# Seven block products for sixteen contraction tiles instead of eight in the second and third pair of output tiles of a down projection

## The chip, the cores and the metric

The kernel runs on one core of one Trainium2 chip. The metric is the device time of one execution in microseconds (us). Three runs of the kernel before took 891.26, 890.07 and 891.31 us, median 891.26.

## The reference

The reference is one layer of a hybrid encoder block over 512 positions of width 1024: two recurrent branches (RWKV-7 and Gated DeltaNet) on one input projection, a gated merge, an output projection with residual, then a gated feed-forward part and a final norm. The change touches only the last product of the feed-forward part:

```python
h = rms_norm(x, norm2_g[l]) @ ffn_up[l]              # 512 x 1024 @ 1024 x 5632
h = causal_depthwise_conv(h, ffn_conv_w[l])
h_gate, h_up = _split(h, (FFN_HIDDEN, FFN_HIDDEN))   # 2816 each
x = x + (jax.nn.silu(h_gate) * h_up) @ ffn_down[l]   # 2816 x 1024
return rms_norm(x, final_g)
```

Everything is float32.

## The kernel before

Activations lie transposed: channels on the 128 partitions, the 512 positions along the free axis. The hidden width 2816 is 22 contraction tiles, the output width 1024 is 8 output tiles, taken in four pairs (`down_pair`, i = 0 to 3).

Each float32 operand is split in two: hi, a rounded copy that ScalarE (ACT) writes, and lo, the rest, subtracted by VectorE (DVE) or GpSimd (POOL). A product is three matmuls: lo weights by hi data, hi by hi, hi by lo. All three add up in PSUM.

The contraction tiles 0 to 7 (four pairs, `NPAIR`) are multiplied by a scheme of Strassen's kind (`seven`): a pair of output tiles, a pair of contraction tiles and the two halves of the positions (a and b, 256 each) make a 2 x 2 by 2 x 2 block product, done with seven block products instead of eight. The weight side needs the blocks A11, A12, A22 and four sums S1 to S4, the data side the blocks B11, B21, B22 and four sums T1 to T4. `pair_operands` builds the data side while the up projection runs (eight tiles, in `uh` and `ul`, `eh`, `el` and the lora buffers). `pair_weights` builds the weight side, for two contraction pairs at a time: one raw buffer of 128 x 1024, filled by two transfers of 256 KB, four sums of 256 columns, four splits. The split weights go into `u2h` and `u2l`, the inputs of the up projection, which are free by then; they hold two such sets.

The contraction tiles 8 to 21 are multiplied plainly (`plain`), with matmuls of 512 columns; their weights come by `unit` and `halves_of`, in parts of 512 columns, through two raw buffers and a ring of four hi and four lo tiles (`HB`).

The order of the work is drawn up ahead of the run by the framework: each instruction goes to its engine's queue by its priority and by when a planner takes its inputs and buffers to be ready; on the chip each engine then runs its queue in that order, with semaphores. Weight loading and splitting is traced at high priority. In the first and third output pair the plain tiles come first and the seven products behind them; in the second and fourth it is the other way round, so that the seven products of two neighbours stand back to back. After the products the blocks are added up out of PSUM (`V`, `W`) into `x1`, and `total` adds the accumulated rows. The last output tile is done in two halves, each with its normalisation and its part of the output transfer.

The lines that the steps touch: `halves_of` (158 hi, 160 lo), `split` (203, 204), `pair_operands` (1018), `pair_weights` (1044 transfers, 1048 sums, 1057 hi, 1058 lo), `mm` (1089), the block sums (1108, 1109), `total` (1135, 1138), the last tile's norm (1163 to 1172).

Of the kernel before, what the change touches and what calls it, by code (L numbers as in the profile page):

```python
# [9 lines left out]
F32 = mybir.dt.float32  # L10
F32R = mybir.dt.float32r
BF16 = mybir.dt.bfloat16
AF = mybir.ActivationFunctionType
ALU = mybir.AluOpType
PSUM = bass.MemoryType.PSUM

T = 512
D = 1024
KD = D // 128
# [3 lines left out]
HB = 4  # L23
TAGS = {"T": 4, "P": 3, "T2": 2}
# [8 lines left out]
NJ = HID // 128  # L33
NPAIR = 4
# [62 lines left out]
class Body:  # L97
# [938 lines left out]
        self.pairs[i] = B  # L1036


    def pair_weights(self, m, s):
        nc = self.nc  # L1040
        with self.tc.high_priority():
            raw = self.stream.tile([128, 1024], F32, tag="raw", name=self.nm("raw"), bufs=2)
            for i in range(2):
                nc.sync.dma_start(out=raw[:, i * 512:i * 512 + 512], in_=self.a["ffn_down"][m + i][:, s * 512:s * 512 + 512])
            A = raw.rearrange("p (m c i t) -> p m i c t", m=2, c=2, i=2)
            s12, s34 = [self.t("P") for _ in range(2)]
            v = lambda t: t.rearrange("p (s c t) -> p s c t", s=2, c=2)
            tt = lambda out, x, y, op: nc.vector.tensor_tensor(out=out, in0=x, in1=y, op=op)
            p = 4 * (self.sets % 2)
            self.sets += 1  # L1050
            h, l = [[t[:, p + q, :] for q in range(4)] for t in (self.u2h, self.u2l)]

            def parts(q, src, w, eng):
                hq, lq = h[q][:, 0:w], l[q][:, 0:w]
                if len(src.shape) == 3:
                    hq, lq = [x.rearrange("p (c t) -> p c t", c=2) for x in (hq, lq)]
                nc.scalar.activation(hq, src, AF.Copy)
                eng.tensor_tensor(out=lq, in0=src, in1=hq.bitcast(F32), op=ALU.subtract)

            parts(0, raw[:, 0:512], 512, nc.gpsimd)  # L1060
            tt(v(s12)[:, 0], A[:, 1, 0], A[:, 1, 1], ALU.add)
            tt(v(s12)[:, 1], v(s12)[:, 0], A[:, 0, 0], ALU.subtract)
            parts(3, A[:, 1, 1], 256, nc.vector)
            tt(v(s34)[:, 1], A[:, 0, 1], v(s12)[:, 1], ALU.subtract)
            tt(v(s34)[:, 0], A[:, 0, 0], A[:, 1, 0], ALU.subtract)
            parts(1, s12, 512, nc.vector)
            parts(2, s34, 512, nc.gpsimd)
        w = {}
        for n, q, f in (("A11", 0, lambda c: 2 * c), ("A12", 0, lambda c: 2 * c + 1), ("A22", 3, lambda c: c),
                        ("S1", 1, lambda c: c), ("S2", 1, lambda c: 2 + c), ("S3", 2, lambda c: c), ("S4", 2, lambda c: 2 + c)):  # L1070
            w[n] = [tuple(t[q][:, f(c) * 128:f(c) * 128 + 128] for t in (h, l)) for c in range(2)]
        return w


    def down_pair(self, i, act, acc):
        nc, tc = self.nc, self.tc
        x1 = self.x1
        H = T // 2
        a, b = slice(0, H), slice(H, T)
        m1 = 2 * i  # L1080
        end = i == KD // 2 - 1
        tags = "DDAA" if i % 2 == 0 else "ABBB"
        rows = [self.bank_of(t) for t in tags[0:2]]
        pc, pd = [self.bank_of(t) for t in tags[2:4]]
        started = set()


        def mm(bank, out, w, x, stop=False):
            nc.tensor.matmul(out, w, x, start=bank not in started, stop=stop)  # L1089
            started.add(bank)  # L1090

        def seven():
            X = {"X1": ("c", pc, a), "X6": ("c", pc, b), "X5": ("d", pd, a), "X7": ("d", pd, b),
                 "X2": ((0, False), rows[0], a), "X3": ((0, False), rows[0], b), "X4": ((1, False), rows[1], a)}
            for s in range(NPAIR // 2):
                w = self.pair_weights(m1, s)
                for A, B, x in (("A11", "B11", "X1"), ("A12", "B21", "X2"), ("A22", "T4", "X4"), ("S1", "T1", "X5"),
                                ("S2", "T2", "X6"), ("S4", "B22", "X3"), ("S3", "T3", "X7")):
                    for c in range(2):
                        (wh, wl), (xh, xl) = w[A][c], self.pairs[2 * s + c][B]  # L1100
                        fin = s == NPAIR // 2 - 1 and c == 1
                        bank, ps, cols = X[x]
                        mm(bank, ps[:, cols], wl, xh)
                        mm(bank, ps[:, cols], wh, xh)
                        mm(bank, ps[:, cols], wh, xl, stop=fin and (x in ("X6", "X7") or i % 2 == 0 and x in ("X3", "X4")))
            V, W = self.t(), self.t()
            with tc.high_priority():
                tt = lambda out, x, y: nc.vector.tensor_tensor(out=out, in0=x, in1=y, op=ALU.add)
                nc.scalar.activation(V[:, a], pc[:, a], AF.Copy)
                tt(V[:, b], pc[:, b], V[:, a])  # L1110
                tt(W[:, a], pd[:, b], V[:, b])
                tt(V[:, b], pd[:, a], V[:, b])
                tt(W[:, b], pd[:, a], W[:, a])
                for j, t in ((0, V), (1, W)):
                    tt(x1[:, m1 + j, :], t, x1[:, m1 + j, :])

        def plain(j, cols=None):
            ps = rows[j]
            for k0, w in ((8, 8), (16, 6)):
                parts = self.unit(self.a["ffn_down"][m1 + j][:, k0 * 128:(k0 + w) * 128], w * 128)  # L1120
                for q, (wh, wl, n) in enumerate(parts):
                    for part, y in ((wl, 0), (wh, 0), (wh, 1)):
                        for k in range(n):
                            kk = k0 + 4 * q + k
                            wk, x = part[:, k * 128:k * 128 + 128], act(kk)[y]
                            fin = kk == NJ - 1 and y == 1 and i % 2 == 1

                            fresh = j == 1 and i % 2 == 1 and q + k + y == 0 and k0 == 8 and part is wl
                            for s in [cols] if cols else [a, b] if fresh else [slice(0, T)]:
                                mm((j, cols == b), ps[:, s], wk, x[:, s], stop=fin)  # L1130

        def total(m, ps, cols=slice(0, T)):
            x = x1[:, m, cols]
            with tc.high_priority():
                nc.vector.tensor_tensor(out=x, in0=ps[:, cols], in1=x, op=ALU.add)
            if m < KD - 1:
                self.sumsq(acc, x, m == 0)
                nc.scalar.activation(x, x, AF.Copy, scale=self.vec("final", m))

        if i % 2 == 0:  # L1140
            plain(0)
            plain(1)
            seven()
            for j in range(2):
                total(m1 + j, rows[j])
            return
        seven()
        plain(0)
        total(m1, rows[0])
        if not end:  # L1150
            plain(1)
            total(m1 + 1, rows[1])
            return

        for cols in (a, b):
            if cols == b:
                rows[1] = self.bank_of("D")
            plain(1, cols)
            m = KD - 1
            total(m, rows[1], cols)  # L1160
            x = x1[:, m, cols]
            sq, r, pn = self.t(), self.t(), self.bank_of("A" if cols == a else "D")
            nc.scalar.activation(sq[:, 0:H], x, AF.Square)
            nc.tensor.matmul(pn[:, 0:H], self.con("ones"), acc[:, cols], start=True, stop=False)
            nc.tensor.matmul(pn[:, 0:H], self.con("ones"), sq[:, 0:H], start=False, stop=True)
            nc.scalar.activation(x, x, AF.Copy, scale=self.vec("final", m))
            nc.scalar.activation(r[:, 0:H], pn[:, 0:H], AF.Sqrt, bias=self.eps("norm"), scale=1.0 / D)
            nc.vector.reciprocal(r[:, 0:H], r[:, 0:H])
            for k0, k1 in OUTG:
                xo = x1[:, k0:k1, cols]  # L1170
                nc.vector.tensor_tensor(out=xo, in0=xo, in1=r[:, 0:H].unsqueeze(1).broadcast_to([128, k1 - k0, H]), op=ALU.mult)
                nc.sync.dma_start(out=self.o["outT"][k0:k1].rearrange("k p t -> p k t")[:, :, cols], in_=xo)

    def mlp(self):
        nc = self.nc
# [3 lines left out]
        H = T // 2  # L1179
# [3 lines left out]
        lo = [el[:, x, :] for x in range(4)]  # L1183
# [1 line left out]
            lo += [t[:, x * H:x * H + H] for x in range(n)]  # L1185
        self.ext = [([eh[:, i, x, :] for x in range(3)], lo[3 * i:3 * i + 3]) for i in range(NPAIR)]
        self.pairs = {}
        self.sets = 0
        acc = self.g2
        act = lambda j: (self.uh[:, j, :], self.ul[:, j, :]) if j < 8 else (ah[:, j - 8, :], al[:, j - 8, :])  # L1190
        held = None
# [67 lines left out]
```

## Time and profile before

| | before |
|---|---|
| median of three runs | 891.26 us |
| the profiled execution | 889.34 us |
| its span, first to last instruction | 887.6 us |
| TensorE (PE) matmul busy | 854.3 us, 96% |
| VectorE (DVE) busy | 653.5 us, 74% |
| ScalarE (ACT) busy | 466.0 us, 53% |
| GpSimd (POOL) busy | 210.3 us, 24% |
| down projection, first to last matmul start | 759.3 to 877.3 us |

Times inside the profile are us from the span's start. Matmuls are pipelined: their durations overlap, so a stream of them is priced by the distance from one start to the next. Idle time is put down to whatever released the instruction that ended it ("<-").

### The profile page before, as it was taken

Reading aid. Unit: us, or ns where it says so; the run is one execution under the profiler, and the core shown is the slowest. Engines: PE = TensorE matmul, PEld = TensorE weight load, DVE = VectorE, ACT = ScalarE, POOL = GpSimd, SP = SyncE. Lnnn points to the kernel's source line nnn. Section 1 sums busy time; section 2 is a strip of 40 time slices with the busy share of each in tenths; the row PEclk is TensorE's granted clock in tenths of the full one; section 3 lists DMA queues with packets and bytes.
Section 4 is the critical chain, followed back from the end, with each engine's and each line's share of the span. In section 5 each row is a group of like instructions: output and inputs, shape, how many; then the busy total and the mean of one; then the engine's idle time right before and its main releaser. Section 6 shows DMA issues by size and latency. Waiting matters only on the chain.

```text
span 887.6 us, 13504 instructions
## 1 busy us (share of the span) xinstructions
PE 854.3 (96%) x5046; PEld 679.3 (77%) x5046; DVE 653.5 (74%) x1247; ACT 466.0 (53%) x905; POOL 210.3 (24%) x189
## 2 busy tenths in 40 slices
PE   8989999999999899999999999999999999999996
PEld 4867677766777677668788878888888888898895
DVE  6899897973899978944577448998866666573665
ACT  7745357666543677573544455554444444443333
POOL 2231123111111221111122212223222222342431
PEclk9999999999999999999999999999999999999998
DMA  7321222212112211136153223332323332332333
GB/s 265 115 89 59 73 71 73 69 57 68 48 60 72 71 50 60 60 109 213 49 194 113 95 72 95 96 95 98 116 95 95 95 96 89 111 104 82 104 87 132
DMA packets 29746, 84.25 MB, mean 95 GB/s; under 512 B 3312, under 2 KB 5488, under 8 KB 29680
## 3 DMA queue, kind: packets, MB, share of 16 engines
q1 hardware_dynamic: 29680, 83.39, 29.6%
q8 instruction: 40, 0.66, 0.3%
q14 instruction: 26, 0.21, 0.1%
HBM read 77.61 MB, written 5.77 MB: 94 GB/s over the span
## 4 chain that ended last, share of the span: by engine, by line
PE 68%; DVE 16%; ACT 6%; issue 3%; POOL 0%; DVEq 0%; ACTq 0%; POOLq 0%
PE D L185 43%; PE D L1089 5%; PE A L1089 4%; PE B L1089 3%; PE B L185 2%; DVE invN L565 2%; PE A L185 2%; DVE invY L567 2%; DVE P L771 1%; DVE lo L160 1%; DVE R L531 1%; DVE BK L510 1%; DVE BK L515 1%; ACT hi L158 1%; PE B L663 1%
## 5 line engine op out<-in xcount | busy, mean ns | idle before, releaser
L160 POOL TENSOR_TENSOR lo<-raw,hi 128x512 fp32r<-128x512 f32 x124 | 170.6, 1376 | 578.4 <-ACT hi L158 577.2
L158 ACT ACTIVATE hi<-raw 128x512 fp32r<-128x512 f32 x248 | 152.7, 619 | 181.4 <-PE D L185 87.2
L185 PE MATMUL D<-uh,lo 128*128 128x512 f32 x384 | 160.5, 418 | 2.7 <-DVE R L375 1.4
L185 PE MATMUL D<-uh,hi 128*128 128x512 f32 x384 | 151.4, 395 | 0.0
L185 PE MATMUL D<-u2h,lo 128*128 128x512 f32 x352 | 137.9, 392 | 0.0
L185 PE MATMUL D<-u2h,hi 128*128 128x512 f32 x352 | 137.8, 392 | 0.0
L160 DVE TENSOR_TENSOR lo<-raw,hi 128x512 fp32r<-128x512 f32 x124 | 88.2, 711 | 46.3 <-ACT hi L158 45.7
L185 PE MATMUL D<-ul,hi 128*128 128x512 f32 x384 | 109.1, 406 | 0.0
L185 PE MATMUL D<-u2l,hi 128*128 128x512 f32 x352 | 95.1, 392 | 0.0
L185 PEld LDWEIGHTS D<-uh,lo 128*128 128x128 f32 x384 | 72.2, 188 | 21.3 <-issue 3.1
L1006 DVE SCALAR_TENSOR_TENSOR P<-T,vecs,P 128x511 f32<-128x511 f32 x88 | 81.8, 929 | 6.9 <-ACT P L1004 2.6
L185 PEld LDWEIGHTS D<-uh,hi 128*128 128x128 f32 x384 | 72.3, 188 | 14.6 <-issue 1.0
L185 PEld LDWEIGHTS D<-ul,hi 128*128 128x128 f32 x384 | 69.3, 188 | 16.3 <-issue 1.0
L185 PEld LDWEIGHTS D<-u2h,hi 128*128 128x128 f32 x352 | 66.1, 188 | 14.9 <-issue 0.2
L185 PEld LDWEIGHTS D<-u2h,lo 128*128 128x128 f32 x352 | 66.1, 188 | 14.7 <-issue 0.2
L185 PEld LDWEIGHTS D<-u2l,hi 128*128 128x128 f32 x352 | 66.1, 188 | 14.1
L1003 DVE TENSOR_TENSOR T<-D,acc 128x512 f32<-128x512 f32 x44 | 30.2, 686 | 32.0 <-PE D L185 28.2
L565 DVE TENSOR_TENSOR invN<-invA,invY 128x60 f32<-128x60 f32 (+24 forms) x124 | 39.6, 319 | 3.0
L1004 ACT ACTIVATE P<-T,vecs 128x512 f32<-128x512 f32 x44 | 31.7, 721 | 16.5 <-DVE T L1003 14.5
L567 DVE TENSOR_TENSOR invY<-invY,invN 128x60 f32<-128x60 f32 (+24 forms) x124 | 32.3, 260 | 3.0
L771 DVE SCALAR_TENSOR_TENSOR P<-D,vecs,P 128x511 f32<-128x511 f32 (+2 forms) x36 | 26.7, 742 | 0.8 <-ACT P L769 0.7
L1195 ACT ACTIVATE P<-P 128x512 f32<-128x512 f32 x22 | 13.7, 624 | 21.0 <-DVE P L1006 21.0
(437 smaller groups left out, 1556.5 us busy)
## 6 DMA issues: line engine op xcount, KB each, us to landing
raw<-w_in SPq DMA_DIRECT2D x44, 512.0 KB, 3.6
raw<-ffn_up SPq DMA_DIRECT2D x44, 512.0 KB, 3.5
raw<-ffn_down SPq DMA_DIRECT2D x9, 512.0 KB, 3.5
raw<-w_out SPq DMA_DIRECT2D x8, 512.0 KB, 3.5
raw<-ffn_down SPq DMA_DIRECT2D x16, 256.0 KB, 2.9
spill<-T SPq DMA_DIRECT2D x14, 256.0 KB, 2.0
R<-spill SPq DMA_DIRECT2D x14, 256.0 KB, 3.9
raw<-ffn_down SPq DMA_DIRECT2D x9, 384.0 KB, 3.1
```

The lines of the kernel that those rows point to most:

```text
L158: nc.scalar.activation(hi[:, 0:w], raw[:, o:o + w], AF.Copy)
L160: self.on(str(self.halves % 4)).tensor_tensor(out=lo[:, 0:w], in0=raw[:, o:o + w], in1=hi[:, 0:w].bitcast(F32), op=ALU.subtract)
L185: nc.tensor.matmul(ps, t[:, w[k]], x[k][p], start=(first and i == 0 and q == 0), stop=(last and i == len(parts) - 1 and q == len(seq) - 1))
L510: nc.vector.scalar_tensor_tensor(out=bkh[h][s, :, sb, :], in0=q(K, s, h), scalar=self.hkk[s, hp:hp + 1], in1=q(at, s, h), op0=ALU.mult, op ...
L565: nc.vector.tensor_tensor(out=w, in0=rows[:, t, 0:t].unsqueeze(2).broadcast_to([128, t, n]), in1=Ym[:, t, c:G].unsqueeze(1).broadcast_to([ ...
L567: nc.vector.tensor_tensor(out=Ym[:, 0:t, c:G], in0=Ym[:, 0:t, c:G], in1=w, op=ALU.add)
L771: nc.vector.scalar_tensor_tensor(out=cv[:, sh:], in0=ps[:, 0:T - sh], scalar=w(3 - sh), in1=cv[:, sh:], op0=ALU.mult, op1=ALU.add)
L1003: nc.vector.tensor_tensor(out=h, in0=ps, in1=self.acc2, op=ALU.mult)
L1004: nc.scalar.activation(cv, h, AF.Copy, scale=w(2))
L1006: nc.vector.scalar_tensor_tensor(out=cv[:, sh:], in0=h[:, 0:T - sh], scalar=w(2 - sh), in1=cv[:, sh:], op0=ALU.mult, op1=ALU.add)
L1089: nc.tensor.matmul(out, w, x, start=bank not in started, stop=stop)
L1195: nc.scalar.activation(g, g, AF.Silu)
```

## The change

- `late_operands` is new. For the contraction tiles 8 to 15 (four more pairs) it adds hi and lo back together, forms T1 to T4 with four subtractions of 256 columns and splits them into `u2h` and `u2l`. B11, B21 and B22 are the tiles that are there already. It is traced in the first output pair, between `plain(0)` and `seven()`.
- The second and third output pair take sixteen contraction tiles by seven products (two sets of four pairs) and six plainly; the first and the fourth stay at eight and fourteen.
- `pair_weights` makes sets of four contraction pairs. It loads one row of 512 KB for each of the two output tiles, each into a raw buffer of its own (both are used), forms four sums of 512 columns (S3 in place in the raw buffer), and splits each of the seven products' weights into a hi and a lo tile of the ring of four. DVE makes four of the seven lo tiles, POOL three.
- The seven products come in the order A11, A12, S1, S2, S3, S4, A22, each over four contraction pairs.
- The first output pair runs `plain(0)`, the seven products, `plain(1)`; the other three run the seven products first.

The diff, cut to its core:

```diff
+    def late_operands(self, i, act):
...
+        k = 2 * i
+        tt = lambda out, x, y, op: nc.vector.tensor_tensor(out=out, in0=x, in1=y, op=op)
+        g = []
+        for q in range(2):
+            g.append(self.work.tile([128, T], F32, tag="BK", name=self.nm("gu"), bufs=2))
+            h, l = act(k + q)
+            tt(g[q], h.bitcast(F32), l.bitcast(F32), ALU.add)
+        t = [self.work.tile([128, T], F32, tag="T2", name=self.nm("late"), bufs=TAGS["T2"]) for _ in range(2)]
+        tt(t[0][:, a], g[0][:, b], g[0][:, a], ALU.subtract)
+        tt(t[1][:, a], g[1][:, b], g[0][:, b], ALU.subtract)
+        tt(t[0][:, b], g[1][:, b], t[0][:, a], ALU.subtract)
+        tt(t[1][:, b], g[1][:, a], t[0][:, b], ALU.subtract)
+        p = 2 * i - 2 * NPAIR
+        B = {}
+        for q in range(2):
+            h, l = self.u2h[:, p + q, :], self.u2l[:, p + q, :]
+            self.split(h, l, t[q])
...
     def pair_weights(self, m, s):
...
-            raw = self.stream.tile([128, 1024], F32, tag="raw", name=self.nm("raw"), bufs=2)
             for i in range(2):
-                nc.sync.dma_start(out=raw[:, i * 512:i * 512 + 512], in_=self.a["ffn_down"][m + i][:, s * 512:s * 512 + 512])
+                raw = self.stream.tile([128, 1024], F32, tag="raw", name=self.nm("raw"), bufs=2)
+                nc.sync.dma_start(out=raw, in_=self.a["ffn_down"][m + i][:, s * 1024:s * 1024 + 1024])
...
+            S1, S2, S4 = [four(self.t("P")) for _ in range(3)]
+            S3 = A[1, 0]
...
+            for n, B, src, o in (("A11", "B11", A[0, 0], "X1"), ("A12", "B21", A[0, 1], "X2"), ("S1", "T1", S1, "X5"),
+                                 ("S2", "T2", S2, "X6"), ("S3", "T3", S3, "X7"), ("S4", "B22", S4, "X3"), ("A22", "T4", A[1, 1], "X4")):
+                if n == "S1":
+                    tt(S1, A[1, 0], A[1, 1], ALU.add)
+                    tt(S2, S1, A[0, 0], ALU.subtract)
+                    tt(S3, A[0, 0], A[1, 0], ALU.subtract)
+                    tt(S4, A[0, 1], S2, ALU.subtract)
+                hi = self.stream.tile([128, 512], F32R, tag="hi", name=self.nm("hi"), bufs=HB)
+                lo = self.stream.tile([128, 512], F32R, tag="lo", name=self.nm("lo"), bufs=HB)
+                nc.scalar.activation(four(hi), src, AF.Copy)
+                (nc.gpsimd if n in ("A11", "S3", "A22") else nc.vector).tensor_tensor(
+                    out=four(lo), in0=src, in1=four(hi).bitcast(F32), op=ALU.subtract)
...
     def down_pair(self, i, act, acc):
...
+        sets = range(2) if 0 < i < KD // 2 - 1 else range(1)
+        K0 = 8 * len(sets)
...
-            for k0, w in ((8, 8), (16, 6)):
+            for k0, w in ((8, 8), (16, 6))[len(sets) - 1:]:
...
-        if i % 2 == 0:
+        if i == 0:
             plain(0)
-            plain(1)
-            seven()
-            for j in range(2):
-                total(m1 + j, rows[j])
-            return
+            for p in range(NPAIR, 2 * NPAIR):
+                self.late_operands(p, act)
         seven()
-        plain(0)
+        if i:
+            plain(0)
         total(m1, rows[0])
```

## Rows read from the trace of the kernel before

**Rows 1.** Busy time by stretch; the columns are named in the first row.

```profile
core 0: us, PE busy (x) PEld busy (x) DVE busy (x) ACT busy (x) POOL busy (x), PEclk, DMA share, GB/s
740.00:759.30 19.30, 19.30 (x86) 15.82 (x85) 12.52 (x17) 8.91 (x14) 5.38 (x4) 1.00 0.32 101
...
759.30:788.50 29.20, 29.20 (x170) 25.73 (x169) 17.41 (x30) 12.22 (x22) 12.32 (x9) 1.00 0.33 104
```

**Rows 2.** Chain of waits from 740 us: start, us, what.

```profile
759.48 19.23 PE D L1089 x84
...
866.59 4.96 PE B L1089 x42
...
871.57 0.43 DVE x L1135
```

**Rows 3.** Waits of PE from 759 us on: us in total, times, longest.

```profile
PE D L1165 <- ACT T L1163: 0.7, 1, 0.7
```

**Rows 4.** Timeline of PE, first pair: start, us, engine, line, operation.

```profile
759.32 0.39 PE L1089 MATMUL D<-ah,lo 128*128 128x512 f32 x1
...
778.54 0.28 PE L1089 MATMUL A<-uh,u2l 128*128 128x256 f32 x1
...
788.49 0.28 PE L1089 MATMUL B<-uh,u2l 128*128 128x256 f32 x1
```

**Rows 5.** Timelines of ACT, DVE, POOL and SP: weight splits and transfers.

```profile
762.31 0.63 ACT L158 ACTIVATE hi<-raw 128x512 fp32r<-128x512 f32 x1 [1.34 <-PE D L1089]
765.67 0.69 DVE L160 TENSOR_TENSOR lo<-raw,hi 128x512 fp32r<-128x512 f32 x1 [0.71 <-ACT hi L158]
768.52 1.30 POOL L160 TENSOR_TENSOR lo<-raw,hi 128x512 fp32r<-128x512 f32 x1 [4.10 <-ACT hi L158]
760.12 0.41 DVE L160 TENSOR_TENSOR lo<-raw,hi 128x256 fp32r<-128x256 f32 x1
760.60 0.33 SPq L169 DMA_DIRECT2D raw<-ffn_down  x1
766.43 0.80 SPq L1044 DMA_DIRECT2D raw<-ffn_down  x2
769.03 0.63 ACT L1057 ACTIVATE u2h<-raw 128x512 fp32r<-128x512 f32 x1 [0.59 <-DMA raw<-ffn_down]
783.59 0.33 SPq L169 DMA_DIRECT2D raw<-ffn_down  x1
787.10 0.63 ACT L158 ACTIVATE hi<-raw 128x512 fp32r<-128x512 f32 x1 [2.71 <-DMA raw<-ffn_down]
```

**Rows 6.** Timeline of DVE, data operands of the fourth contraction pair.

```profile
611.27 0.69 DVE L204 TENSOR_TENSOR ul<-gu,uh 128x512 fp32r<-128x512 f32 x1
611.87 0.42 DVE L1018 TENSOR_TENSOR t<-gu,gu 128x256 f32<-128x256 f32 x1
612.20 0.68 DVE L204 TENSOR_TENSOR ul<-gu,uh 128x512 fp32r<-128x512 f32 x1
```

**Rows 7.** Timelines of DVE and POOL where both have work.

```profile
778.37 0.67 DVE L1058 TENSOR_TENSOR u2l<-P,u2h 128x512 fp32r<-128x512 f32 x1
778.85 2.35 POOL L1058 TENSOR_TENSOR u2l<-P,u2h 128x512 fp32r<-128x512 f32 x1 [2.37 <-ACT u2h L1057]
...
779.64 0.41 DVE L1048 TENSOR_TENSOR P<-raw,P 128x256 f32<-128x256 f32 x1
...
837.47 1.34 POOL L1058 TENSOR_TENSOR u2l<-P,u2h 128x512 fp32r<-128x512 f32 x1 [2.03 <-ACT u2h L1057]
837.58 1.51 DVE L1048 TENSOR_TENSOR P<-P,raw 128x256 f32<-128x256 f32 x1
...
849.21 1.47 POOL L1058 TENSOR_TENSOR u2l<-P,u2h 128x512 fp32r<-128x512 f32 x1
849.45 0.41 DVE L1108 TENSOR_TENSOR T<-A,T 128x256 f32<-128x256 f32 x1
```

**Rows 8.** Timeline of DVE, the last hidden tile.

```profile
761.00 1.54 DVE L1006 SCALAR_TENSOR_TENSOR P<-T,vecs,P 128x511 f32<-128x511 f32 x2 [0.46 <-ACT P L1004]
```

More of the change, by code (lines that the diff above doesn't have):

```diff
@@ L1036, in pair_operands @@
         self.pairs[i] = B
+    def late_operands(self, i, act):
+        nc = self.nc
+        H = T // 2
+        a, b = slice(0, H), slice(H, T)
+        k = 2 * i
[15 more added lines that the diff above has]
+            self.split(h, l, t[q])
+            for n, c in zip((("T1", "T2"), ("T3", "T4"))[q], (a, b)):
+                B[n] = (h[:, c], l[:, c])
+        for n, q, c in (("B11", 0, a), ("B21", 1, a), ("B22", 1, b)):
+            B[n] = tuple(x[:, c] for x in act(k + q))
+        self.pairs[i] = B
@@ L1039, in pair_weights @@
     def pair_weights(self, m, s):
         nc = self.nc
+        A = {}
+        w = []
         with self.tc.high_priority():
-            raw = self.stream.tile([128, 1024], F32, tag="raw", name=self.nm("raw"), bufs=2)
             for i in range(2):
-                nc.sync.dma_start(out=raw[:, i * 512:i * 512 + 512], in_=self.a["ffn_down"][m + i][:, s * 512:s * 512 + 512])
-            A = raw.rearrange("p (m c i t) -> p m i c t", m=2, c=2, i=2)
-            s12, s34 = [self.t("P") for _ in range(2)]
@@ L1047, in pair_weights @@
-            v = lambda t: t.rearrange("p (s c t) -> p s c t", s=2, c=2)
-            tt = lambda out, x, y, op: nc.vector.tensor_tensor(out=out, in0=x, in1=y, op=op)
[L1049 to L1071, printed above, removed]
+                raw = self.stream.tile([128, 1024], F32, tag="raw", name=self.nm("raw"), bufs=2)
@@ new lines, in pair_weights @@
+                nc.sync.dma_start(out=raw, in_=self.a["ffn_down"][m + i][:, s * 1024:s * 1024 + 1024])
+                v = raw.rearrange("p (c i t) -> p i c t", c=4, i=2)
+                A[i, 0], A[i, 1] = v[:, 0], v[:, 1]
+            four = lambda t: t.rearrange("p (c t) -> p c t", c=4)
+            S1, S2, S4 = [four(self.t("P")) for _ in range(3)]
+            S3 = A[1, 0]
+            tt = lambda out, x, y, op: nc.vector.tensor_tensor(out=out, in0=x, in1=y, op=op)
+            for n, B, src, o in (("A11", "B11", A[0, 0], "X1"), ("A12", "B21", A[0, 1], "X2"), ("S1", "T1", S1, "X5"),
[10 more added lines that the diff above has]
+                    out=four(lo), in0=src, in1=four(hi).bitcast(F32), op=ALU.subtract)
+                w.append((B, o, hi, lo))
@@ L1094, in seven @@
                  "X2": ((0, False), rows[0], a), "X3": ((0, False), rows[0], b), "X4": ((1, False), rows[1], a)}
[L1095 to L1102, printed above, removed]
+            for s in sets:
+                for B, x, hi, lo in self.pair_weights(m1, s):
+                    bank, ps, cols = X[x]
+                    for c in range(4):
+                        wh, wl = [t[:, c * 128:c * 128 + 128] for t in (hi, lo)]
+                        xh, xl = self.pairs[4 * s + c][B]
+                        fin = s == sets[-1] and c == 3
                         mm(bank, ps[:, cols], wl, xh)
                         mm(bank, ps[:, cols], wh, xh)
-                        mm(bank, ps[:, cols], wh, xl, stop=fin and (x in ("X6", "X7") or i % 2 == 0 and x in ("X3", "X4")))
+                        mm(bank, ps[:, cols], wh, xl, stop=fin and x in (("X6", "X7") if i else ("X6", "X7", "X3")))
             V, W = self.t(), self.t()
@@ L1125, in plain @@
                             wk, x = part[:, k * 128:k * 128 + 128], act(kk)[y]
-                            fin = kk == NJ - 1 and y == 1 and i % 2 == 1
-                            fresh = j == 1 and i % 2 == 1 and q + k + y == 0 and k0 == 8 and part is wl
+                            fin = kk == NJ - 1 and y == 1 and i + j > 0
+                            fresh = j == 1 and q + k + y == 0 and k0 == K0 and part is wl
                             for s in [cols] if cols else [a, b] if fresh else [slice(0, T)]:
@@ L1187, in mlp @@
         self.pairs = {}
-        self.sets = 0
         acc = self.g2
```

## The prediction

> **What bounds the kernel now.** I read the stages first [rows 1]: before and in the down projection TensorE (PE) is busy for the whole of each stretch at a granted clock of 1.00 (2.4 GHz), while VectorE (DVE) and GpSimd (POOL) together are busy for as long as the stretch in the first two output pairs' plain tiles and products. The chain of waits [rows 2] says the same from the end backwards: from 759 us to 871.6 us it is matmuls alone; behind them stands the normalisation of the last output tile, which the change leaves as it is. PE's own list of waits from 759 us on has one entry, 0.7 us, and it lies in that tail [rows 3]. So in this stretch the end moves only by matmul time, and by whatever newly fails to be ready for PE.
>
> The matmuls are priced by start to start, since their durations overlap. 84 matmuls of 512 columns start between 759.32 and 778.54: 228.8 ns each. 84 of 256 columns start between 778.54 and 788.49: 118.5 ns each [rows 4]. Half the columns cost 4.1 ns more than half the time.
>
> **Step 1, matmuls: -2.05 us.** Eight contraction tiles (four pairs) of one pair of output tiles cost 2 x 8 x 3 = 48 matmuls of 512 columns, 10.98 us. As seven products they are 4 x 7 x 3 = 84 of 256 columns, 9.95 us. The saving is 1.03 us, for two pairs of output tiles 2.06; two plain runs now begin with a split first matmul (0.01 us each). No other matmul is added or removed. The Trainium skill ("TensorE: Matmul & The Clock Gate", Back-to-back issue gap) puts warm spacing at columns / 2.4 GHz plus 2.5 ns: estimated 109.2 and 215.8 ns, and a saving of 1.19 us per output pair, 2.4 in all; both rows are slower than it says and the rows decide.
>
> **Step 2, weight sets of four pairs: +0.9 us.** One product of a set is now 12 matmuls, 1.42 us, a set 9.95 us. Its weights pass through the ring of four hi and lo tiles that the plain runs use, where before a whole set stood ready in u2h and u2l. A new hi tile can be written when the product four places earlier is through; an ACT copy starts about 0.25 us after the last such matmul (part over at 762.06, copy at 762.31, 0.63 us), the lo subtraction takes 0.69 us on DVE or 1.30 on POOL [rows 5]. From slot to lo tile that is about 2.2 us where 4.27 (three products) are there: hidden inside a set, and from plain to set.
>
> What is late is the turn from one set to the next. The two raw buffers hold both weight rows of a set. The second row is read until the last product, A22, is split. A22 needs the slot of S1, the third product: free at 3 x 1.42 + 0.25 = 4.5 us after the set's start; copy to 5.15, POOL to 6.5. Then SP issues the next 512 KB at 6.6 (0.07 us after the releasing lo, 760.60 behind 760.53), which is there 3.5 us later (issued 783.59, its reader starts 787.10) [rows 5]: at 10.1. Then DVE forms four sums of 512 columns at 0.60 each, in the order of the code, before S1's lo: 12.5, and with 0.69 and a handover 13.2. PE wants S1 after the next set's A11 and A12, at 9.95 + 2.84 = 12.8. That is 0.45 us late, at the two places where a set follows a set (inside the second and the third output pair): 0.9 us. Bounds: nothing, if the data comes after 2.6 us as the first 256 KB piece did (issued 766.43, reader at 769.03); up to 1.5 us each if POOL's lo of A22 is held by DVE as below. I take the middle value because its row is of the same size of transfer. Turns from a set to plain tiles are covered: the first row's buffer is free early.
>
> **Step 3, late operands: +0.7 us.** Per contraction pair two additions, four half-width subtractions and two splits: DVE starts such 512-wide operations 0.60 us apart and 256-wide ones 0.34 apart [rows 6], so 2 x 0.60 + 4 x 0.34 + 2 x 0.60 = 3.76 us, 15.0 for four; ACT's eight copies (5 us) find room, as ACT is busy 12.2 of 29.2 us there. The question is DVE and POOL. When both read SBUF they exclude each other: a POOL subtraction of 1.3 us lasts 2.35 while DVE runs four such operations from 778.37 to 780.05 behind each other, and a DVE one of 0.41 started behind POOL's at 837.47 lasts 1.51, to just after POOL's end; one that reads PSUM (849.45) still takes 0.41 beside POOL [rows 7]. The two engines' SBUF work must therefore be added up. From 759.3 to the first set of the second output pair's S1 (788.5 + 2.84 = 791.4, 32.1 us) stand in line:
> the last hidden tile 2.8 (1.54 for two operations [rows 8], a product and a split at 0.6 to 0.7); the end of plain(0)'s weights 0.4; the first set, 8 DVE operations x 0.60 + 3 of POOL x 1.30 = 8.7; late operands 15.0 less what runs earlier; plain(1)'s weights 2 x 1.30 + 0.60 + 0.34 = 3.5; two additions into x1 1.2; of the next set A11, A12, four sums and S1's lo 4.9.
> The first late pair (2.56 us until its splits, which must wait for u2h and u2l) and the additions of the second (1.20) need only tiles 8 to 11 and free buffers, so they can lie in DVE's gaps before 759 (DVE 12.5 and POOL 5.4 busy of 19.3 us [rows 1] leave 1.4 free; five such stretches pass after tile 11 is there): 3.8. The sum is 36.5 - 3.8 = 32.7 for 32.1; with 0.1 for handovers I take 0.7. Behind that S1 nothing more is lost: what is left of its set, the next set's A11 and A12 and one addition ask 6.3 of 7.1 us. Bounds: nothing, if handovers overlap a little more; and above, if nothing runs early (+3.8) and PSUM reads (0.69 + 4 x 0.34 + 2 x 0.69 = 3.4 us in this stretch) find no cover, 7.9 us. I take the low side, because the operand code of the earlier pairs did fill DVE's row without a gap when it was ready [rows 6] and because PSUM reads go beside POOL [rows 7].
>
> **Sum.** -2.05 + 0.9 + 0.7 = -0.45 us. The profiled execution took 889.34 us (span 887.6 and 1.7 around it), so 888.9 by its measure; it lies 1.9 below the median of the runs, 891.26, and on that scale the forecast is 890.8.
>
> **Rivals.** *Clean gain.* The turn and the late operands are both hidden: -2.05, 889.2. For it: PE waits nowhere in this stretch today although the sets of the first two output pairs stood back to back with DVE and POOL together busy for 29.7 of 29.2 us (both counts hold waiting) [rows 1]; one POOL subtraction fewer per set of four also relieves both. Against: today's double set in u2h and u2l gives the lead that is now given up.
> *DVE and POOL overrun (slower).* The late operands don't start before 759, or stand in DVE's queue ahead of the lo tiles of the first sets, which wait behind them in order: A12's, S1's, S2's and S4's lo, and POOL's A22 behind DVE's run. Then 36.5 us of work meet 32.1: 4.4 us of PE waiting, at the end of the first set, in plain(1) or at the second output pair's first set. With the turn's 0.9: -2.05 + 0.9 + 4.4 = +3.25, 894.5; with uncovered PSUM reads 897.9. It makes the kernel slower from the point where the work ahead of that S1 exceeds 33.3 us (32.1 + 2.05 - 0.9). Against: gaps before 759. The Trainium skill ("SBUF — State Buffer", SBUF: two separate sides) states that whichever of the two engines starts first keeps the shared ports for its whole instruction and the other blocks fully; the trace agrees (1.51 for 0.41), and in the 2.35 us case POOL was held over several instructions.
> *It does less than it says.* If 256-column matmuls of the late pairs came at more than 130.7 ns (10.98 / 84) the saving would be gone: then +1.6, 892.9. Against: all 84 spacings of rows 4 are even; for it nothing.
>
> **How the numbers follow.** A measurement of this kernel can tell about 0.2%, 1.8 us, from no change. The clean gain just exceeds that: chance 0.2. The forecast, with its own range of 889.6 to 893.0, has 0.47, the failed saving 0.03: both are within 0.2%. The overrun has 0.3; nearly all of it is slower by more than 0.2%. So faster 0.2, same 0.5, slower 0.3. The range that holds the time 8 times in 10 takes in the clean gain and most of the overrun: 889.0 to 895.5.
>
> **What would show it.** Step 1: 168 more matmuls of 256 columns and 96 fewer of 512 (but the split ones), at the spacings above. Step 2: PE idle some 0.4 us before S1's lo of the second set, in the second and third output pairs, released by DVE, and ahead of it DVE's sums released by the raw transfer. Step 3: DVE rows of the additions before 759 us, and little PE idle time between 769 and 800 us. Wrong would be: idle PE of several us in that stretch behind lo tiles (overrun); no idle PE at all (clean gain); a wait at any other turn, from a set to plain tiles or at a PSUM bank, which I have at nothing since the banks of one output pair are read out a whole pair before they return.

## The result and the profile after

The changed kernel takes 896.06 us, the median of four runs (895.68 to 896.72), against 890.66 us for the kernel before (four runs, 889.38 to 891.31). The ratio is 1.0064 with a 95% interval of 1.0047 to 1.0081: 5.4 us slower. The time lies just above the range of 889.0 to 895.5, in the span of the rival that was called overrun (894.5, up to 897.9).

| | before | after |
|---|---|---|
| the profiled execution | 889.34 us | 896.72 us |
| its span | 887.6 us | 894.9 us |
| first matmul of the down projection | 759.3 us | 761.4 us |
| from there to the span's end | 128.3 us | 133.5 us |
| matmul instructions | 5046 | 5120 |

Of the 7.3 us between the two spans, 2.1 are there by 548 us already (the first data operand of L1018 starts at 548.4, before at 546.3), ahead of the change's first instruction at 626 us: they are a difference between two executions (TensorE's granted clock is 0.89 from 60 to 75 us and 0.83 from 225 to 235 us in the profile of after, and 1.00 in both stretches of before's). So only the last stretch is compared: 133.5 against 128.3, +5.2 us, close to the 5.4 of the medians. This length, called the segment below, is the span less the start of the first down-projection matmul in the same profile.

Start with what PE waits for, in the profile after, from 740 us on (columns: us in total, times, longest). [rows 3] had the ACT line alone, and it is still there in the tail; the other five are new.

```profile
PE A L1113 <- POOL lo L1091: 2.2, 1, 2.2
PE A L1113 <- DVE lo L1091: 0.8, 1, 0.8
PE D L1186 <- ACT T L1184: 0.7, 1, 0.7
PE D L1113 <- ACT ah L203: 0.6, 1, 0.6
PE D L1113 <- DVE al L204: 0.5, 1, 0.5
PE B L1113 <- DVE lo L1091: 0.4, 1, 0.4
```

The timeline of PE in the profile after (start, us, engine, line, operation, and in brackets the idle time and its releaser) says where three of them are. It answers to [rows 4].

```profile
769.64 0.39 PE L1113 MATMUL D<-ah,lo 128*128 128x512 f32 x1
770.59 0.50 PE L1113 MATMUL D<-ah,lo 128*128 128x512 f32 x1 [0.56 <-ACT ah L203]
...
772.34 0.50 PE L1113 MATMUL D<-al,hi 128*128 128x512 f32 x1 [0.55 <-DVE al L204]
772.67 0.28 PE L1113 MATMUL A<-uh,lo 128*128 128x256 f32 x1
...
778.17 0.28 PE L1113 MATMUL A<-lora_l,hi 128*128 128x256 f32 x1
780.63 0.39 PE L1113 MATMUL A<-eh,lo 128*128 128x256 f32 x1 [2.18 <-POOL lo L1091]
...
782.01 0.41 PE L1113 MATMUL A<-eh,lo 128*128 128x256 f32 x1
782.23 0.41 PE L1113 MATMUL A<-eh,hi 128*128 128x256 f32 x1
...
785.10 0.28 PE L1113 MATMUL D<-eh,lo 128*128 128x256 f32 x1
```

The pauses are the distances from start to start beyond the usual ones (0.229 and 0.117 us): 0.72 + 0.11 us at 770.59 and 0.71 + 0.10 at 772.34 (the second figure is the slower first matmul behind each pause), and 2.34 + 0.10 at 780.63. From 781.6 us on, 0.9 us behind that pause, the matmuls come 0.213 us apart instead of 0.117, until 784.8. Busy time by stretch in the same profile, answering to [rows 1], with the columns named there:

```profile
740.00:761.40 21.40, 21.40 (x96) 17.54 (x94) 16.45 (x22) 10.93 (x18) 5.54 (x4) 1.00 0.32 93
761.40:780.60 19.20, 15.94 (x91) 13.30 (x89) 19.16 (x35) 9.68 (x17) 7.32 (x3) 1.00 0.19 56
780.60:785.10 4.50, 4.47 (x25) 4.47 (x26) 4.16 (x7) 1.26 (x2) 3.10 (x2) 0.62 0.32 87
785.10:795.00 9.90, 9.90 (x53) 8.42 (x52) 6.03 (x11) 3.56 (x6) 2.58 (x2) 1.00 0.36 106
```

In the second stretch DVE is busy for 19.16 of 19.20 us and PE for only 15.94. In the third, PE has a granted clock of 0.62, which is mostly the 1.2 GHz level, soon after a pause of 2.34 us: 24 distances took 4.47 us instead of 2.81.

The chain of waits of after (start, us, what), which answers to [rows 2], shows the big pause and the first turn from set to set (`P` and `raw` at L1080 are the weight sums).

```profile
775.04 5.55 POOL lo L1091
...
780.63 2.23 PE A L1113 x12
...
801.25 1.31 POOL lo L1091
802.58 3.41 DMA raw<-ffn_down
...
806.09 0.70 DVE P L1080
...
808.71 2.31 DVE lo L1091 x2
...
811.06 3.10 PE B L1113 x24
```

One POOL subtraction of 1.3 us ([rows 5]) takes 5.55. It is the lo tile of S3 in the first set, issued at 775.04, while PE asks for it at 778.3. DVE's timeline in after says what it stood beside, and how late the last hidden tile was (its product at 769.20, its split at 771.60).

```profile
764.42 0.68 DVE L204 TENSOR_TENSOR u2l<-late,u2h 128x512 fp32r<-128x512 f32 x1
...
769.20 0.68 DVE L1217 TENSOR_TENSOR P<-P,P 128x512 f32<-128x512 f32 x1
...
771.60 0.68 DVE L204 TENSOR_TENSOR al<-P,ah 128x512 fp32r<-128x512 f32 x1
...
775.02 0.68 DVE L1044 TENSOR_TENSOR gu<-ah,al 128x512 f32<-128x512 f32 x1
775.62 0.41 DVE L1044 TENSOR_TENSOR late<-gu,late 128x256 f32<-128x256 f32 x1
...
777.76 0.68 DVE L1091 TENSOR_TENSOR lo<-P,hi 128x512 fp32r<-128x512 f32 x1
...
779.04 0.41 DVE L1044 TENSOR_TENSOR late<-gu,late 128x256 f32<-128x256 f32 x1
779.48 1.37 DVE L1044 TENSOR_TENSOR late<-gu,late 128x256 f32<-128x256 f32 x1
```

From 775.02 to 779.04 each DVE instruction starts 0.34 or 0.60 us after the one before it, with no pause, and all read two operands from SBUF. The next one starts 0.44 us later, at 779.48, and takes 1.37 us instead of 0.41; POOL's ends at 780.58. The last hidden tile is split at 771.60, 10.2 us after the down projection's first matmul. In before that was 4.6 (763.96 against 759.32):

```profile
763.96 1.00 DVE L204 TENSOR_TENSOR al<-P,ah 128x512 fp32r<-128x512 f32 x1 [0.70 <-ACT ah L203]
```

There, between that first matmul and this split, DVE's queue held one weight lo of 0.41 us (760.12, [rows 5]) and no weight sum beside the tile's own work. In after it held late operands, three of the four weight sums and a weight lo as well.

All of it together: -2.05 (fewer matmul columns) - 0.75 (504 matmuls of 256 columns, now 117.0 ns apart instead of 118.5) + 1.64 (last hidden tile) + 2.44 + 1.56 (POOL's S3, and the half clock behind it: 4.47 - 2.81 less the 0.10 already counted) + 1.0 and 1.3 (the turns at 809.36 and 838.69) = +5.1, against 5.2 in the segments.

### The profile page after: what moved, and what is told of

Same layout as the page of the kernel before. It is cut to its first block, busy times and chain, and to the rows that moved or that the text cites. A ratio compares the mean times of both kernels' runs of the same rounds, so it can differ in the third digit from the quotient of the medians.

```text
span 894.9 us, 13704 instructions
## 1 busy us (share of the span) xinstructions
PE 858.2 (96%) x5120; PEld 684.3 (76%) x5120; DVE 679.4 (76%) x1275; ACT 471.8 (53%) x915; POOL 209.8 (23%) x187
## 5 line engine op out<-in xcount | busy, mean ns | idle before, releaser
L160 POOL TENSOR_TENSOR lo<-raw,hi 128x512 fp32r<-128x512 f32 x120 | 164.5, 1370 | 546.4 <-ACT hi L158 546.4
L158 ACT ACTIVATE hi<-raw 128x512 fp32r<-128x512 f32 x240 | 147.3, 617 | 129.6 <-PE D L185 56.4
L160 DVE TENSOR_TENSOR lo<-raw,hi 128x512 fp32r<-128x512 f32 (+1 forms) x120 | 86.9, 724 | 36.0 <-ACT hi L158 35.2
L1006 DVE SCALAR_TENSOR_TENSOR P<-T,vecs,P 128x511 f32<-128x511 f32 x88 | 91.0, 1034 | 5.9 <-ACT P L1004 3.2
L1091 POOL TENSOR_TENSOR lo<-raw,hi 128x512 fp32r<-128x512 f32 x18 | 29.2, 1622 | 54.6 <-ACT hi L1090 54.5
```

The costliest lines, as they stand in the source:

```text
L158: nc.scalar.activation(hi[:, 0:w], raw[:, o:o + w], AF.Copy)
L160: self.on(str(self.halves % 4)).tensor_tensor(out=lo[:, 0:w], in0=raw[:, o:o + w], in1=hi[:, 0:w].bitcast(F32), op=ALU.subtract)
L1006: nc.vector.scalar_tensor_tensor(out=cv[:, sh:], in0=h[:, 0:T - sh], scalar=w(2 - sh), in1=cv[:, sh:], op0=ALU.mult, op1=ALU.add)
L1091: (nc.gpsimd if n in ("A11", "S3", "A22") else nc.vector).tensor_tensor(out=four(lo), in0=src, in1=four(hi).bitcast(F32), op=ALU.subtract)
```

## The experiments

Theory O (order): the late operands cost by where they stand. They lie in DVE's in-order queue ahead of the last hidden tile, and they make a DVE run without pauses beside which POOL's lo tile is held. Theory S (sum): DVE and POOL simply have too much work up to the second pair's first set. Theory W (weights): sets of four through a ring of four are what is slow. In the expectations, theory A is that the late operands' DVE work is the loss (O and S together), theory B is W, the order theory is O and the sum theory S. All kernels below are the changed kernel with the edit shown, unless another is named. Each ratio of e1 to e10 is to the kernel before, timed in the same five rounds; those of e1 to e4, of e5 to e8 and of e9 and e10 ran on three chips, and after's ratio is that of the result. So a run is compared with after, or with a run of another group, by the two ratios to before. An interval is some 0.12 points to either side (0.17 for after and e6), so two ratios must lie about 0.2 points, 1.8 us, apart to differ in time; smaller differences are read from the traces.

| kernel | median, before (us) | ratio and interval | segment (us) |
|---|---|---|---|
| after | 896.06, 890.66 | 1.0064 [1.0047, 1.0081] | 133.5 |
| e1, sets of four only | 890.62, 889.62 | 1.0009 [0.9997, 1.0020] | 128.0 |
| e2, late operands unused | 896.86, 889.62 | 1.0072 [1.0060, 1.0084] | 132.1 |
| e3, no additions | 895.62, 889.62 | 1.0058 [1.0045, 1.0070] | 131.4 |
| e4, raw row free early | 895.47, 889.62 | 1.0055 [1.0043, 1.0067] | 132.9 |
| e5, first set's lo on DVE | 892.75, 890.20 | 1.0023 [1.0012, 1.0034] | 130.8 |
| e6, late behind the last tile | 894.84, 890.20 | 1.0050 [1.0033, 1.0068] | 131.7 |
| e7, late operands spread | 892.32, 890.20 | 1.0026 [1.0014, 1.0038] | 130.3 |
| e8, e7 and e4 | 892.11, 890.20 | 1.0021 [1.0008, 1.0034] | 129.0 |
| e9, e8 for the third pair only | 889.76, 890.17 | 0.9994 [0.9982, 1.0005] | 127.0 |
| e10, e4, e5 and e6 | 891.09, 890.17 | 1.0012 [1.0001, 1.0024] | 129.4 |

### e1: sets of four pairs, eight tiles in every output pair, no late operands

```diff
-        sets = range(2) if 0 < i < KD // 2 - 1 else range(1)
+        sets = range(1)
...
-            for p in range(NPAIR, 2 * NPAIR):
-                self.late_operands(p, act)
```

> The weight sets of four pairs and the new order of the first and third output pair, without late operands: every output pair takes eight contraction tiles by seven products and fourteen plainly, so the matmuls are those of the kernel before. Theory A (the loss comes from the late operands' DVE work in the first output pair): same as before, 0 to 1 us faster, since in the changed kernel's trace 256-column matmuls come 1.5 ns closer (336 x 1.5 = 0.5 us), and no PE wait in the first output pair. Theory B (the loss comes from the ring of four tiles and the two raw buffers): slower than before by 1 us or more, with PE waiting for lo tiles at the beginning or end of a set.

PE waits for nothing but the tail's 0.7 us, and the interval of the ratio holds 1. POOL's lo of S3 takes what it should in its timeline:

```profile
775.10 1.29 POOL L1091 TENSOR_TENSOR lo<-raw,hi 128x512 fp32r<-128x512 f32 x1 [6.88 <-ACT hi L1090]
```

Theory W falls: the new weight path alone, where no set follows a set, costs nothing that can be told.

### e2: e1 with the late operands formed, and not used

```diff
-        sets = range(2) if 0 < i < KD // 2 - 1 else range(1)
+        sets = range(1)
```

> As the run before it, but the late operands are formed in the same place; nothing reads them, no product uses them. Theory A: slower than the run before it by 4 to 6 us, in the same three places as the changed kernel: two waits for the last hidden tile (0.8 us each) and one of about 2.3 us for a lo tile of POOL, with a stretch at half clock behind it. Theory B: same as the run before it within 1 us.

It is 0.63 points (5.6 us) slower than e1, and as slow as after. But for the two turns from set to set, which it does not have, PE's waits in this profile are those of after, to the figure: 2.2 us for POOL's lo, 0.6 for ah, 0.5 for al. POOL's two subtractions take 6.98 us instead of 2.6:

```profile
776.80 6.98 POOL L1091 TENSOR_TENSOR lo<-raw,hi 128x512 fp32r<-128x512 f32 x2 [7.52 <-ACT hi L1090]
```

Forming the operands is the loss, whether they are used or not. The segments of e1 and e2 differ by 4.1 us, the sum of the pauses, and the granted clock stays at 1.00 behind them (776 to 790 us). That e2 is as slow as after is in part chance: what after saves by its matmuls (2.3 us against e2) it loses at the turns. The times of e1 and e2 differ by more than 4.1. A half clock in other executions could make up the rest, but that is not shown: timed runs leave no trace, and the mean granted clock on record, 0.993 in e1 and 0.992 in e2 at the median, hardly differs.

### e3: T1 to T4 from the hi tiles alone (the lo part is left out of them)

```diff
-            g.append(self.work.tile([128, T], F32, tag="BK", name=self.nm("gu"), bufs=2))
-            h, l = act(k + q)
-            tt(g[q], h.bitcast(F32), l.bitcast(F32), ALU.add)
+            g.append(act(k + q)[0].bitcast(F32))
```

> The changed kernel without the eight additions of hi and lo: the late operands are formed from the hi tiles alone (the lo part is left out of T1 to T4). DVE has 4.8 us less to do, 2.4 of it behind 759 us. Theory A: faster than the changed kernel by 2 to 4 us, with POOL's longest hold below 5.5 us. Theory B: no difference above 0.5 us.

Eight DVE additions less (4.8 us of work) gave 2.1 us in the segment and no difference that the times can tell from after: a miss. PE's waits show why. The wait for POOL is gone, but the last hidden tile comes no earlier: its split starts at 770.68, again 10.2 us after the down projection's first matmul (760.44), behind late subtractions and splits. The two waits for it have become one, and the first turn (second line) grew:

```profile
PE D L1111 <- DVE al L204: 1.4, 1, 1.4
PE B L1111 <- DVE lo L1089: 1.2, 1, 1.2
```

So work taken away is not gain by its amount, which speaks against S as the whole story. Its median is 6.0 us above before's and its segment only 3.1: in the profile 1.1 us more lie ahead of the segment, and the profiled execution (893.58 us) was 2.0 us shorter than the median. Why the others were longer stays open.

### e4: the second raw row free early

```diff
-                                 ("S2", "T2", S2, "X6"), ("S3", "T3", S3, "X7"), ("S4", "B22", S4, "X3"), ("A22", "T4", A[1, 1], "X4")):
+                                 ("S3", "T3", S3, "X7"), ("A22", "T4", A[1, 1], "X4"), ("S2", "T2", S2, "X6"), ("S4", "B22", S4, "X3")):
```

> The changed kernel with the products in the order A11, A12, S1, S3, A22, S2, S4: the second raw row is then read to its end two products earlier (A22's hi slot comes free at 1.7 us after the set's start, not at 4.5), and the next transfer can land some 2.8 us earlier. Both theories expect the waits at the two turns from set to set (1.0 and 1.3 us in the changed kernel) to go: 2.0 to 2.4 us faster than the changed kernel. The 5.7 us in the first output pair should stay (theory A); theory B has them fall too, since the ring is read in another order.

Both turn waits are gone, so the raw row is their cause. But S3 now comes one product earlier in the first set, and PE's wait for POOL there grew; its granted clock in the 5 us behind it is 0.66 (columns as above):

```profile
PE A L1113 <- POOL lo L1091: 3.6, 1, 3.6
```

```profile
781.00:786.00 5.00, 5.00 (x33) 5.00 (x32) 2.54 (x3) 2.30 (x4) 1.69 (x2) 0.66 0.28 79
```

What was won at the turns was lost here, and the 2.0 to 2.4 us expected did not come.

### e5: S3's and A22's lo tiles of the first set on DVE

```diff
-                (nc.gpsimd if n in ("A11", "S3", "A22") else nc.vector).tensor_tensor(
+                (nc.gpsimd if n in (("A11", "S3", "A22") if m else ("A11",)) else nc.vector).tensor_tensor(
```

> The changed kernel, but in the first output pair's set the lo tiles of S3 and A22 are made by DVE instead of POOL (DVE's row is 1.2 us longer, POOL's 2.6 us shorter). If POOL being shut out by DVE's unbroken run is what PE waits for (order theory), the 2.3 us wait and the half-clock stretch behind it (1.8 us) go and the two waits for the last hidden tile stay: 3 to 4 us faster than the changed kernel. If it is the sum of the two engines' SBUF work (sum theory), only the 1.4 us that POOL's two operations are dearer is gained.

The clearest run: DVE, the busier engine, got two more instructions (1.2 us), and the kernel is 0.41 points (3.7 us) faster than after. PE no longer waits for POOL; what is left are the last hidden tile and the turns.

```profile
PE B L1113 <- DVE lo L1091: 1.2, 1, 1.2
...
PE A L1113 <- DVE lo L1091: 0.7, 1, 0.7
PE D L1113 <- ACT ah L203: 0.6, 1, 0.6
PE D L1113 <- DVE al L204: 0.5, 1, 0.5
```

### e6: the late operands on DVE behind the last hidden tile

```diff
-            self.on("p").tensor_tensor(out=lo, in0=src, in1=hi.bitcast(F32), op=ALU.subtract)
+            self.mark = self.on("p").tensor_tensor(out=lo, in0=src, in1=hi.bitcast(F32), op=ALU.subtract)
...
+            with self.tc.issue_after(mark.ins) if i == NPAIR else nullcontext():
+                self.split(h, l, t[q])
...
+            mark = self.mark
...
+                with tc.issue_after(mark.ins) if p > NPAIR else nullcontext():
+                    self.late_operands(p, act)
```

> The changed kernel with the late operands' DVE instructions put behind the last hidden tile's in DVE's queue (only the first pair's additions and subtractions stay before it). No work is added or removed. Order theory: the two waits for the last hidden tile (1.6 us) go, and what happens to the POOL wait depends on where DVE's row is broken; 1.5 to 5 us faster than the changed kernel. Sum theory: the work ahead of the second output pair's first set is the same or more, so PE waits as long, only later: no faster.

The waits for ah and al are gone, and the tile is split 4.6 us after the first matmul again, as in before: the queue order was their cause. What was moved behind the tile makes the same kind of DVE run there, and POOL is held as in after, in DVE's and POOL's timelines:

```profile
764.14 1.01 DVE L204 TENSOR_TENSOR al<-P,ah 128x512 fp32r<-128x512 f32 x1 [0.70 <-ACT ah L203]
```

```profile
771.48 7.21 POOL L1093 TENSOR_TENSOR lo<-raw,hi 128x512 fp32r<-128x512 f32 x2 [6.88 <-ACT hi L1092]
```

PE waits 2.4 us for it. The segment is 1.8 us shorter than after's; the times can't tell the two apart, so the 1.5 to 5 us expected are not shown in them. e4, e5 and e6 each remove one place and leave the others: the three places are separate.

### e7 and e8: one late pair per plain stretch, sixteen tiles in the third and fourth output pair

```diff
+        def late(p):
+            with tc.issue_after(self.mark.ins) if p > NPAIR else nullcontext():
+                self.late_operands(p, act)
...
-        sets = range(2) if 0 < i < KD // 2 - 1 else range(1)
+        sets = range(2) if i > 1 else range(1)
...
+        if i == 1:
+            late(NPAIR + 2)
...
+        if i < 2:
+            late(NPAIR + 1 + 2 * i)
```

> The late operands serve the third and the fourth output pair instead of the second and third, and are spread: one contraction pair in each of four plain stretches (behind the last hidden tile, behind the first pair's block sums and first total, behind the second pair's), held there by DVE's queue. Matmuls as in the changed kernel. Both theories: no PE wait in the first output pair, so the changed kernel less 5.7 us; the waits at the two turns from set to set stay (2.3 us). Against the kernel before: -2.8 (168 matmuls fewer of the long kind and closer spacing) + 2.3, about -0.5 us.

> As the run before it, with the products in the order A11, A12, S1, S3, A22, S2, S4, which took the waits at the turns away in an earlier run: no PE wait for weights at all, -2.0 to -2.8 us against the kernel before, and 2 us faster than the run before it.

PE has no wait left in the first two output pairs: the same work, spread out, is hidden. Up to the last matmul of the down projection e7 is 0.4 us shorter than before and e8 1.9 (117.5 and 116.1 us from the first to the last, before 118.0). Yet both are slower than before in the times, which was not expected, and e7's chain of waits shows the reason at the very end:

```profile
878.15 0.44 DVE x L1160
...
879.08 0.71 PE D L1195 x2
...
880.33 1.75 DVE T L1198
882.08 0.55 DVE x L1201
...
883.22 3.61 DVE x L1201 x6
```

With sixteen tiles in sets, the last output tile has 6 plain tiles instead of 14. Its second half's 18 matmuls, instead of 42, no longer cover the first half's normalisation, and all eight output multiplications, of both halves, run behind the last norm; in before four do. From the second half's total to the span's end it takes 12.5 us (878.15 to 890.6); in before it was 9.7 (877.89 to 887.6), by its chain:

```profile
877.89 0.34 DVE x L1135
...
883.05 1.20 DVE x L1171 x2
```

e8, with e4's order as well, is 1.3 us shorter in the segment and the same in the times; one turn wait of 0.4 us is left, and its tail is like e7's.

### e9: the third output pair alone

The edit to e8:

```diff
-        sets = range(2) if i > 1 else range(1)
+        sets = range(2) if i == 2 else range(1)
```

> As the run with spread late operands and the early freed row, but only the third output pair takes sixteen contraction tiles by seven products; the fourth is as in the kernel before, so the last tile's normalisation of its first half lies beside as many matmuls again. If the 1.9 us that the spread kernels are slower than the kernel before come from that tail (in their traces no wait is left in the first two output pairs), this one is 0.5 to 1.6 us faster than the kernel before: -1.03 for the matmuls, -0.6 for the closer spacing of 420 matmuls, up to +1 for one turn. If not, it stays slower than before.

One turn wait of 0.2 us is left, and the old tail. The segment is 127.0 us, 1.3 under before's, about what one output pair saves (1.03 by [rows 4], 0.6 for the closer spacing, less 0.4 for the turn). In the times it can't be told from before: 0.9994 [0.9982, 1.0005]. The saving is there in the one trace and too small for the times to show.

### e10: the three cures on the change itself

e4, e5 and e6 together, with sixteen tiles in the second and third output pair as in the change.

> The changed kernel with the three single cures together: late operands' DVE instructions behind the last hidden tile's, the first set's S3 and A22 lo tiles by DVE, and the products in the order that frees the second raw row early. Second and third output pair as in the changed kernel, all late work as before. Order theory: each cure takes its own wait away and none is left above 0.3 us: 1.5 to 2.8 us faster than the kernel before. Sum theory: the late work is still too much for the time before the second output pair's second set, so a wait of 1 to 4 us appears there, and the kernel is at best the same as before.

It is 0.52 points (4.6 us) faster than after and still not faster than before. PE's waits up to 810 us, and POOL's row:

```profile
PE D L1115 <- POOL lo L160: 1.0, 1, 1.0
PE B L1115 <- DVE lo L1093: 0.5, 1, 0.5
```

```profile
777.20 5.82 POOL L160 TENSOR_TENSOR lo<-raw,hi 128x512 fp32r<-128x512 f32 x2 [11.08 <-ACT hi L158]
```

With the first set's tiles served in time, the plain tile behind it is late, again a POOL subtraction beside a DVE run, and small pauses of 0.15 to 0.25 us follow at 797 to 801. From 781 to 801 us that is some 2.2 us in all, and the 0.5 us of the second line is at the second pair's turn (805.42), 0.7 with the slow restart. This is what S expected and not what O did, and DVE's row has no gap here (columns as above; busy holds the time that POOL keeps DVE waiting):

```profile
771.00:781.00 10.00, 9.63 (x83) 9.43 (x81) 10.00 (x21) 6.03 (x11) 3.80 (x1) 1.00 0.33 94
781.00:791.00 10.00, 9.37 (x42) 7.75 (x43) 10.00 (x16) 4.19 (x8) 3.31 (x3) 1.00 0.35 105
```

So in this order the four late pairs do not fit into this stretch. Whether another order or share between DVE and POOL would fit them in was not tried; e7 to e9, which spread them over later output pairs, hide them. Of the 1 us of e10's 129.4 that is left, 0.9 lies behind the last matmul: from the issue of the last output transfer to the span's end it takes 4.2 us (886.23 to 890.4), in before 3.2 (884.32 to 887.6). Why is not shown.

## Why the prediction was wrong

**Step 1, matmuls (-2.05): the mechanism right, the size 0.75 us short.** 74 more matmuls: 168 of 256 columns for 96 of 512, and two split ones. The 256-wide ones also came 1.5 ns closer, in e1 too, which gave the 0.75 us more; why they did is not shown.

**Step 2, turns (+0.9): the mechanism right, the size off.** The chain at 801 to 811 us is the one that was worked out, link by link: POOL's A22, the transfer (3.41 us for the 3.5 taken), DVE's four sums, then S1's lo. e4 shows its cause by removing it. It cost 1.0 and 1.3 us, inside the bounds of 0 to 1.5 each. The 0.45 counted only the first late tile (0.57 and 0.95 measured); S2's lo was 0.22 and 0.16 late behind it, and each restart cost another 0.11.

**Step 3, late operands (+0.7): this is the step that failed.** It measured 5.6 us: 1.64 for the last hidden tile, 2.44 for POOL's S3, 1.56 for the half clock behind it. That some of the work would run early was right: the first late pair's additions and subtractions ran at 626 to 642 us and the second's additions at 649 and 660. So the sum of 32.7 us for 32.1 was not far off as a sum, though too low: e10, with the three places cured, still loses 2.2 us in the stretch where it gave 0.7. What was wrong above all is to price a filler by a sum. It takes for granted that each engine does next what PE needs next, but DVE's queue was already written, with late operands, weight sums and weight lo tiles ahead of the last hidden tile, and POOL, the engine with time to spare, was not free to use it. [rows 7] held the evidence: one POOL subtraction drawn out to 2.35 us by four DVE instructions. The text read it as a reason to add the two engines up; it should have been read as a delay of one tile, growing with the length of the DVE run, that PE would ask for within 3.3 us.

**The rival.** Overrun named the place (late operands ahead of the lo tiles in DVE's queue, POOL behind DVE's run, the end of the first set) and 4.4 us of waiting; the pauses there are 4.1. That the two figures agree is luck: the 4.4 is the sum of all the work (36.5) less the time there is (32.1), with nothing done before 759 us, though the 3.8 us of additions and subtractions were done by then; the 4.1 is one held POOL tile and the last hidden tile. It lost to the forecast because its price was tied to the sum of work, which seemed to fit. Not foreseen by either: the half clock, and the last hidden tile.

**Clean gain and the failed saving.** The saving by fewer columns is there in full, so the saving did not fail; neither the turns nor the late operands were hidden, so the gain was not clean.

## What to carry to other kernels

Price work that is to fill gaps by whom it holds up, not by its total time: list what stands behind it in the same in-order queue, and which tile on the other engine is wanted within the length of its run. Where VectorE has a long run of instructions that read two operands from SBUF, give the next tile TensorE needs to VectorE itself, though it is the busier engine (e5), or spread the run over later stages (e7 to e9). And when work is taken off the last stage, look first at what that work was hiding (e7's tail).

## What the runs showed of the hardware

- POOL was held for much more than one DVE instruction: 5.55 us for a 1.30 us subtraction, over nine DVE starts without a pause. The Trainium skill ("SBUF — State Buffer", SBUF: two separate sides) says that the engine which starts first has the shared ports for the whole instruction; what happens when further DVE instructions follow without a pause it does not say. Had POOL's turn come behind the one DVE instruction that was running (0.68 us), it would have been done some 2 us after 775.04, and PE would not have waited; the trace shows otherwise.
- The long holds ended alike: POOL was done 1.1 to 1.2 us after the end of the last DVE instruction ahead of a break in DVE's row. In after, e2, e3 and e4 the break is a pause of 0.03 to 0.04 us (in after between 779.45 and 779.48, 780.58 the end of POOL's), in e6 and e10 an instruction that reads PSUM (776.05 and 780.38). In shorter holds POOL got in behind the DVE instruction that was running, with no pause recorded (in after 765.76 to 767.52, where the next DVE instruction then takes 1.78 us). What decides between the two is not settled.
- A long PE pause does not always bring the half clock. In the profiles of after (2.34 us of pause) and e4 (3.74) the granted clock fell to 0.62 and 0.66 for some 5 us; in those of e2 (2.37) and e6 (2.60) it stayed at 1.00. In the eight profiles without a pause above 1.6 us there, it did not fall between 750 and 870 us.
- The first matmul of 256 columns behind a pause puts the next one 0.22 us away instead of 0.117, even where the pause was only 0.15 us (e10, 797.12).
